# Five staging buffers for the modulation weights, and gated-linear outputs stored whole, in a hybrid GLA and retention layer

## The chip, the cores and the metric

The kernel runs on one core of one Trainium2 chip. The metric is device time in microseconds of one execution. The kernel before takes 1753.43 us, the median of 3 runs (1752.35 to 1753.49). All arithmetic is float32; matmul operands are stored as pairs of a rounded high part and the remainder, so that one product becomes three matmuls (high by high, low by high, high by low).

## The reference

One layer with two parallel branches over 1024 prompt tokens and 8 x 4 sample tokens (32 beside the prompt, 1056 in all), model width 1024. Cut to what matters:

```python
shift, scale, gate = split(c @ w_ada + b_ada, 3)        # modulation, 9 conditions: prompt, 8 samples
h = x * (1 + scale) + shift
qg, kg, vg, zg, lr, qr, kr, vr, zr, mg, mr = split_in(h @ w_in)
o_g, s_gla_new = gla(qg * GLA_DK**-0.5, kg, vg, log_alpha, s_gla)   # 4 heads, dk 128, dv 256
o_g = head_rmsnorm(o_g) * gla_norm_g * silu(zg)                     # "gated-linear output"
o_r, s_ret_new = retention(rotary(qr), rotary(kr), vr, s_ret)       # 4 heads, dk 256, dv 512, chunks of 128
o_r = head_groupnorm(o_r) * ret_norm_g * silu(zr)
merged = sigmoid(mg) * (o_g @ w_branch_gla) + sigmoid(mr) * (o_r @ w_branch_ret)
y = layernorm(DEEPNORM_ALPHA * x + gate * (merged @ w_out))
```

The outputs are y and both new states, for prompt and sample.

## The kernel before, in words

**Three stages.** `project` computes `h @ w_in`, `attend` the retention branch, the branch products and the rest. The line numbers are those of the profile of the kernel before.

**The start of `project`.** x (transposed) is in eight tiles `xt` of [128, 2, 528]; two of them (j and j + 4) make one quarter of the operands. For each of the eight tiles a piece of the modulation weights (`ada`, 1 MB in two DMAs of 512 KB) is loaded by SP (`load_ada`, three buffers in turn), PE makes the modulation product of 8 matmuls (`ada`, L508), ACT copies it (`fin`, `mod`, L514), PE transposes it (L517), DVE adds the bias, and `hcalc` scales and shifts the x tile (two small DVE operations and one ACT operation, L527). `combos` then makes the operands from two scaled tiles: the projection multiplies 2 x 2 blocks by a scheme of seven products (P1 to P7), each of which needs its own sum of x blocks. There are seven operands `XH[i]`/`XL[i]`: high part by ACT (`hi`, L541), remainder by DVE (`lo`, L545), sums by DVE (`sums`, L537, in tiles `S`). `first(j)` multiplies one quarter of P2, P1 and P5 as soon as it is there. A loop of eleven rounds writes this in order: modulation product i, copy and scaling of tile i - 1, half of the combos of a pair, the next loads.

**The loop of the projection.** 44 groups of weight columns (NG), seven products each, in the order P2, P1, P5, P6, P3, P4, P7. A group has four blocks of raw weights (`load_raw`, L135, SP), four sums of them (`tsum`, L146, POOL), and each product's weights are split into `wh`/`wl` three products ahead (`parts`, L94/L95 by `split`). PE runs it at L169 (`prod`); ACT and DVE take the results out of PSUM (`outs`, `C` tiles) after P1, P5, P6, P3, P4 and P7, and later functions store the columns.

**Work laid beside the projection.** From group NP1 on, `Q.units`, a list of small functions for the gated linear attention (`gla_units`), is run beside the products: `want` says how many of them must be done after product n, so that all are done 12 products ahead of the end. Its function `gated` transposes the normed output, multiplies it by the gate (`of`), splits it (`ox`, 32 prompt and 4 sample blocks) and stores both parts to DRAM (`og_d[0]`, `og_d[1]`). After the last unit `Q.late` is opened, the list of `early`: loads for the first retention head, its first scores (A0), two copies, and `R.SP`, which prepares the sample tokens' operands (`kd`, `kdr`, `vst`, `A4r`). One of them is run after every second product; what is left runs after the last.

**The junction to `attend`.** `attend` opens its pools, loads the two parts of the gated-linear outputs (4.3 MB each) from DRAM by four POOL DMAs into `og` (four of six `o4` buffers), and calls `begin()` of `branch`, which loads and splits the first branch weights (`wunit`: SP DMA L1195, split). `stage` then runs the retention head in eight chunks of 128 tokens and fills PE with the branch products (`fill`, L1238 to L1240, 352 columns each). For each chunk a retention state of the samples is split by ACT and POOL (`spl`, `ar`), `C1` and `C2` compute scores and output (`o`), `S0` is the first sample product (it reads `A4r` and `vst`). In every chunk but the first head's first, `spl` comes ahead of C1.

**What sets the order.** Each engine runs its instructions in the order in which the code writes them, and waits on semaphores for the others; DMAs of a queue are issued in the order in which their engine reaches them. A buffer of a pool is written again once its last readers are done; a pool that is opened over a closed one waits for the tiles that lay there.

Of the kernel before, what the change touches and what calls it, by code (L numbers as in the profile page):

```python
# [18 lines left out]
P = 128  # L19
# [26 lines left out]
def hybrid_step(ctx: ExitStack, tc: tile.TileContext, a: dict):  # L46
# [44 lines left out]
    og_d = [dp.tile([P, 8, TA], F32, name=f"ogd{i}") for i in range(2)]  # L91
# [16 lines left out]
    def project(early):  # L108
        with ExitStack() as cx:
            xp = pool(cx, "xp")  # L110
            wp = pool(cx, "wpb")
            ps = cx.enter_context(tc.tile_pool(name="psb", bufs=1, space=PSUM))
            _project(xp, wp, ps, early)

    def _project(xp, wp, psp, early):
        XH, XL = {}, {}
        for i in (1, 3, 2, 5, 4, 0, 6):
            XH[i] = xp.tile([P, 4, HT], F32R, name=f"xh{i}")
            XL[i] = xp.tile([P, 4, HT], F32R, name=f"xl{i}")
        mem = SimpleNamespace(cx=None, pool=None, bufs=0)  # L120

        def open_mem(name, bufs):
            mem.cx = ExitStack()
            mem.pool = pool(mem.cx, name)
            mem.bufs = bufs
# [367 lines left out]
        open_mem("su", 0)  # L493
# [38 lines left out]
        def sums(j, k):  # L532
            h0, h1 = xs[j], xs[j + 4]
            x, y, op = {1: lambda: (h0[:, 1], h1[:, 1], add), 2: lambda: (S[1], h0[:, 0], sub),
                        4: lambda: (h1[:, 0], S[2], sub), 3: lambda: (h0[:, 0], h0[:, 1], sub)}[k]()
            S[k] = sup.tile([P, HT], F32, tag="S", name="S", bufs=2)
            nc.vector.tensor_tensor(S[k], x, y, op=op)  # L537

        def hi(j, *ops):
            for i, src in ops:  # L540
                nc.scalar.activation(XH[i][:, j, :], src, AF.Copy)  # L541

        def lo(j, *ops):
            for i, src, eng in ops:
                eng.tensor_tensor(XL[i][:, j, :], src, XH[i][:, j, :].bitcast(F32), op=sub)  # L545

        def combos(j, half):
            h0, h1 = xs[j], xs[j + 4]
            V = nc.vector
            if half == 0:  # L550
                hi(j, (1, h1[:, 0]), (0, h0[:, 0]))
                sums(j, 1)
                lo(j, (1, h1[:, 0], V))
                hi(j, (4, S[1]))
                lo(j, (0, h0[:, 0], V))
                sums(j, 2)
                lo(j, (4, S[1], V))
            else:
                hi(j, (5, S[2]), (3, h1[:, 1]))
                lo(j, (3, h1[:, 1], V))  # L560
                sums(j, 4)
                lo(j, (5, S[2], V))
                hi(j, (2, S[4]))
                sums(j, 3)
                lo(j, (2, S[4], V))
                hi(j, (6, S[3]))
                lo(j, (6, S[3], V))

        nc.vector.tensor_scalar(bada[:, 1, :], bada[:, 1, :], 1.0, None, op0=add)
        for i in range(3):  # L570
            load_ada(i)
            load_x(i)
            if i == 1:
                load_raw(0, ((1, 0), (0, 0), (0, 1), (1, 1)))
# [10 lines left out]
        for i in range(11):  # L585
            if i < 8:
                ada(i)
                if i + 3 < 8:
                    load_ada(i + 3)
            if 0 < i <= 8:  # L590
                fin(i - 1)
            if i == 1:
# [4 lines left out]
            if i >= 3:  # L597
                combos(seq[(i - 3) // 2 * 2], (i - 3) % 2)
            if 0 < i <= 8:
                hcalc(i - 1)  # L600
                if i + 2 < 8:
                    load_x(i + 2)
            if i % 2 == 0 and i > 3:
                first(seq[i - 4])
# [19 lines left out]
        for n, (g, i) in enumerate(flat):  # L624
# [30 lines left out]
            if Q.late:  # L655
                if n % 2 and Q.late[0]:
# [973 lines left out]
```

## Time and profile before

| | before |
|---|---|
| median of 3 runs | 1753.43 us |
| the profiled execution | 1751.33 us |
| its span (first to last instruction) | 1749.6 us |
| PE busy | 1671.3 us |
| mean granted PE clock | 0.984 |

The profile is of one execution. Busy times count an instruction from its start to its end; the share of an engine is its busy time by the span. The page cuts the span into 40 slices of 43.7 us and prints each engine's busy share in tenths. A group's row gives line, engine, operation, tile written from tiles read, count, busy time and mean ns, then the idle time ahead of it and what ended it. "PEclk" or the clock of a window is the granted clock of TensorE, 1.00 at full speed. "SPq" and "POOLq" rows are DMAs issued by those engines' queues, with the time in which they were under way. The engine and page rows that the argument needs stand in the prediction.

### The profile page before, as it was taken

The numbers are of one execution on the slowest core, as the hardware profiler recorded it, in microseconds if no ns is written. First come the engines' busy times: TensorE is split into PE (matmuls) and PEld (weight loads), VectorE is DVE, ScalarE is ACT, GpSimd is POOL, SyncE is SP. The second block draws the span as 40 slices with busy tenths as digits, with TensorE's granted clock in tenths as the row PEclk, the third lists the DMA queues.
The fourth block names the chain that finished last, engine by engine and source line by source line (L and its number), as shares of the span: only waits on it lengthen the run. The fifth ranks groups of instructions, "written<-read, shape, count | busy, mean of one in ns | idle before, by whom it ended". The sixth has DMA issues, their size and how long they took to land.

```text
span 1749.6 us, 32388 instructions
## 1 busy us (share of the span) xinstructions
PE 1671.3 (96%) x11848; PEld 1552.5 (89%) x11848; DVE 1150.3 (66%) x2278; ACT 840.5 (48%) x1819; POOL 697.8 (40%) x791
## 2 busy tenths in 40 slices
PE   7899989999999999999999999799999999998997
PEld 4799989999999999999999999699898788887775
DVE  4647777677765666656576555365676878877557
ACT  4556555543335656556565555333355545434201
POOL 1115656334443343333333332132334444445516
PEclk9999999999999999999999999799999999999998
DMA  8213434543336555555554545766655555447613
GB/s 320 95 50 129 139 127 152 166 137 127 114 113 165 160 165 149 164 148 144 172 152 144 159 146 196 284 193 193 201 159 167 170 171 169 147 123 230 208 37 113
DMA packets 242671, 275.41 MB, mean 157 GB/s; under 512 B 54147, under 2 KB 171472, under 8 KB 242000
## 3 DMA queue, kind: packets, MB, share of 16 engines
q1 hardware_dynamic: 226288, 216.27, 39.9%
q0 software_dynamic: 11872, 48.42, 8.7%
q10 hardware_dynamic: 4352, 8.65, 1.4%
q8 instruction: 93, 1.52, 0.4%
q14 instruction: 66, 0.54, 0.1%
HBM read 176.80 MB, written 96.47 MB: 156 GB/s over the span
## 4 chain that ended last, share of the span: by engine, by line
PE 38%; DVE 4%; POOL 4%; DMA 4%; issue 3%; ACT 2%; POOLq 0%; DVEq 0%; ACTq 0%; SPq 0%
PE psA L169 6%; PE psC L169 4%; PE mm L1239 3%; PE mm L1238 3%; PE mm L1240 3%; PE aux L738 3%; PE o L738 3%; PE psB L169 2%; PE psD L169 2%; PE mm L1453 1%; PE mm L1455 1%; PE mm L1454 1%; PE so L1132 1%; DMA wraw<-wo 1%; POOL acc L1400 1%
## 5 line engine op out<-in xcount | busy, mean ns | idle before, releaser
L169 PE MATMUL psA<-xh,wh 128*128 128x264 f32 x1056 | 306.0, 290 | 8.4 <-ACT C L205 4.7
L169 PE MATMUL psA<-xl,wh 128*128 128x264 f32 x1056 | 301.0, 285 | 1.0 <-DVE xl L545 1.0
L169 PE MATMUL psA<-xh,wl 128*128 128x264 f32 x1056 | 301.4, 285 | 0.5 <-DVE wl L95 0.5
L146 POOL TENSOR_TENSOR T<-raw 128x512 f32<-128x512 f32 x88 | 126.1, 1433 | 214.9 <-DVE wl L95 188.7
L169 PEld LDWEIGHTS psA<-xh,wh 128*128 128x128 f32 x1056 | 199.9, 189 | 12.0 <-ACT C L205 5.8
L146 POOL TENSOR_TENSOR T<-raw,T 128x512 f32<-128x512 f32 x88 | 119.3, 1356 | 226.1 <-issue 161.0
L169 PE MATMUL psC<-xh,wh 128*128 128x264 f32 x704 | 201.9, 287 | 0.3 <-ACT C L210 0.3
L169 PEld LDWEIGHTS psA<-xl,wh 128*128 128x128 f32 x1056 | 200.2, 190 | 1.2 <-DVE xl L545 1.2
L169 PEld LDWEIGHTS psA<-xh,wl 128*128 128x128 f32 x1056 | 200.0, 189 | 0.8 <-DVE wl L95 0.7
L169 PE MATMUL psC<-xl,wh 128*128 128x264 f32 x704 | 199.8, 284 | 0.5 <-DVE xl L545 0.5
L169 PE MATMUL psC<-xh,wl 128*128 128x264 f32 x704 | 200.0, 284 | 0.0
L94 ACT ACTIVATE wh<-raw 128x512 fp32r<-128x512 f32 x180 | 113.0, 630 | 150.7 <-PE psC L169 43.1
L95 DVE TENSOR_TENSOR wl<-raw,wh 128x512 fp32r<-128x512 f32 x180 | 135.9, 755 | 60.8 <-ACT wh L94 57.1
L95 DVE TENSOR_TENSOR wl<-T,wh 128x512 fp32r<-128x512 f32 x176 | 125.4, 713 | 62.9 <-ACT wh L94 58.0
L94 ACT ACTIVATE wh<-T 128x512 fp32r<-128x512 f32 x176 | 110.7, 629 | 105.9 <-PE psA L169 72.5
L1238 PE MATMUL mm<-oh,wh 128*128 128x352 f32 x384 | 128.1, 334 | 7.6 <-DVE acc L1398 6.0
L169 PEld LDWEIGHTS psC<-xh,wh 128*128 128x128 f32 x704 | 132.5, 188 | 1.5 <-issue 0.8
L169 PEld LDWEIGHTS psC<-xl,wh 128*128 128x128 f32 x704 | 132.6, 188 | 0.7 <-DVE xl L545 0.7
L169 PEld LDWEIGHTS psC<-xh,wl 128*128 128x128 f32 x704 | 132.6, 188 | 0.0
L95 POOL TENSOR_TENSOR ar<-s0p,ar 128x512 fp32r<-128x512 f32 x64 | 83.6, 1306 | 107.1 <-ACT ar L94 105.8
L1240 PE MATMUL mm<-oh,wl 128*128 128x352 f32 x384 | 124.8, 325 | 0.0
L1239 PE MATMUL mm<-ol,wh 128*128 128x352 f32 x384 | 124.6, 324 | 0.0
(313 smaller groups left out, 4640.2 us busy)
## 6 DMA issues: line engine op xcount, KB each, us to landing
raw<-wx SPq DMA_DIRECT2D x176, 256.0 KB, 3.1
s0p<-state_ret POOLq DMA_DIRECT2D x32, 512.0 KB, 4.5
o_srs<-s0p POOLq DMA_DIRECT2D x32, 512.0 KB, 3.9
raw<-wb SPq DMA_DIRECT2D x48, 256.0 KB, 3.9
thd<-C ACTq DMA_DIRECT2D x16, 528.0 KB, 3.6
og<-ogd POOLq DMA_DIRECT2D x4, 2112.0 KB, 11.5
thl<-thd SPq DMA_DIRECT2D x48, 176.0 KB, 3.4
ada<-wada SPq DMA_DIRECT2D x16, 512.0 KB, 7.1
```

The costliest lines, as they stand in the source:

```text
L94: nc.scalar.activation(hi, src, AF.Copy)
L95: (eng or nc.vector).tensor_tensor(lo, src, hi.bitcast(F32), op=sub)
L146: nc.gpsimd.tensor_tensor(t, x, y, op=sub)
L169: nc.tensor.matmul(ps[:, :SUB], w[:, j, :], x[:, j, c], start=start and j == 0 and i == 0, stop=stop and j == 3 and i == 2, skip_group_che ...
L738: nc.tensor.matmul(out, lhs(l), rhs(r), start=start and i == 0, stop=stop and i == 2)
L1132: nc.tensor.matmul(R.po[:64], qp[:, d].rearrange("p l t -> p (l t)"), R.ar[:, l, :], start=False, stop=b == 7 and d == 1 and l == 1)
L1238: nc.tensor.matmul(ps, wh[:, j, :], oh[:, j, g0:g1], start=first, stop=False)
L1239: nc.tensor.matmul(ps, wh[:, j, :], ol[:, j, g0:g1], start=False, stop=False)
L1240: nc.tensor.matmul(ps, wl[:, j, :], oh[:, j, g0:g1], start=False, stop=last)
L1400: nc.gpsimd.tensor_tensor(A, A, m0, op=add)
L1453: nc.tensor.matmul(ps, xh, wh[:, k, :], start=k == 0, stop=False)
L1454: nc.tensor.matmul(ps, xh, wl[:, k, :], start=False, stop=False)
```

## The change

The diff does four things.

1. **Start.** Two more buffers for modulation weights (`ada3`, `ada4` in a pool `more`); five pieces and four x tiles are asked for ahead of the first product, in turn. The pool is closed in round 4; operand 6 (`xh6`, `xl6`) and the projection's weight buffers (`wpb`) are placed there afterwards, so the first raw weights, their sums and the first three weight splits move from rounds 0 and 1 to round 4. The combos are made in pieces, their sums in place (in one `S` tile, and the last in the x tile itself). The operands' quarters of pairs 2 and 3 come after the loop of now eight rounds, with `first(2)` and `first(3)`.
2. **Pace at the end of the projection.** The units are spread to be done 13 products ahead of the end instead of 12; the list of `early` has three rests and one function is taken after every product.
3. **Gated-linear outputs.** `gated` stores `of` as it is (one tensor `og_d`, two buffers of `of`), without a split. `attend` loads it by eight POOL DMAs of 528 KB into two `ograw` tiles and splits each eighth into `og` behind `begin()`, ahead of the first head's `stage`. The tiles `oh`/`ol` of the first head come after that, in the buffers of `ograw`.
4. **`kst` and S0.** `kst` moves to another pool (`wc`), and the first head's `S0` stands behind C1 and C2 of its first chunk.

```diff
-    og_d = [dp.tile([P, 8, TA], F32, name=f"ogd{i}") for i in range(2)]
+    og_d = dp.tile([P, 8, TA], F32, name="ogd")
...
+        operands(xp, (1, 3, 2, 5, 4, 0))
...
+        cy = ExitStack()
+        more = pool(cy, "more")
         def load_ada(i):
-            r = raws[i] = sup.tile([P, 2, 4, 256], F32, tag="ada", name="ada", bufs=3)
+            if i % 5 < 3:
+                r = sup.tile([P, 2, 4, 256], F32, tag="ada", name="ada", bufs=3)
+            else:
+                r = more.tile([P, 2, 4, 256], F32, name=f"ada{i}")
+            raws[i] = r
...
+            if what == 0:
+                hi(j, 1, h1[:, 0])
+                hi(j, 0, h0[:, 0])
+                s = S[j] = sup.tile([P, HT], F32, tag="S", name="S", bufs=2)
+                ssum(s, h0[:, 1], h1[:, 1], add)
+                lo(j, 1, h1[:, 0])
+                hi(j, 4, s)
+                lo(j, 0, h0[:, 0])
+                lo(j, 4, s)
+            elif what == 5:
+                ssum(S[j], S[j], h0[:, 0], sub)
+                hi(j, 5, S[j])
+                lo(j, 5, S[j])
...
+        for i in range(8):
+            ada(i)
+            if i + 5 < 8:
+                load_ada(i + 5)
+            if i:
                 fin(i - 1)
+            if i == 4:
+                cy.close()
+                operands(pool(cx, "xp6"), (6,))
+                wp = pool(cx, "wpb")
+                load_raw(0, ((1, 0), (0, 0), (0, 1), (1, 1)))
                 tsum(0, 1)
                 for k in range(3):
                     parts(0, k)
                 tsum(0, 2)
             if i >= 3:
+                j = (i - 3) // 2
+                for w in ((0,), (5, 2, 3, 6))[(i - 3) % 2]:
+                    combos(j, w)
+            if i:
                 hcalc(i - 1)
+            if i < 4:
+                load_x(i + 4)
+            if i in (4, 6):
+                first(i // 2 - 2)
...
+        fin(7)
+        hcalc(7)
+        first(2)
+        combos(3, 0)
+        first(3)
+        for w in (5, 2, 3, 6):
+            combos(2, w)
+            combos(3, w)
...
-                if n % 2 and Q.late[0]:
+                if Q.late[0]:
...
-                want = min(len(Q.units), len(Q.units) * (n + 1 - Q.first) // (len(flat) - Q.first - 12))
+                want = min(len(Q.units), len(Q.units) * (n + 1 - Q.first) // (len(flat) - Q.first - 13))
...
-                of = wk.tile([P, 2, n], F32, tag="of", name="of", bufs=1)
+                of = wk.tile([P, 2, n], F32, tag="of", name="of", bufs=2)
                 nc.vector.tensor_tensor(of, pv, z, op=mult)
-                ox = wk.tile([P, 2, 2, n], F32R, tag="ox", name="ox", bufs=1)
-                split(ox[:, 0], ox[:, 1], of)
-                for i in range(2):
-                    for sl, d0 in dsts:
-                        nc.sync.dma_start(og_d[i][:, 2 * h:2 * h + 2, d0:d0 + sl.stop - sl.start],
-                                          ox[:, i, :, sl].bitcast(F32))
+                for sl, d0 in dsts:
+                    nc.sync.dma_start(og_d[:, 2 * h:2 * h + 2, d0:d0 + sl.stop - sl.start], of[:, :, sl])
...
-            kst = AT.wb.tile([P, DK_R], F32R, tag="kst", name="kst", bufs=2)
+            kst = AT.wc.tile([P, DK_R], F32R, tag="kst", name="kst", bufs=2)
...
+        rest = lambda: None
+        return [loads, rest, rest, lambda: R.A0(0), rest, lambda: R.CPa(0), lambda: (R.CPv(0), R.ldv(2)), R.SP]
...
-            og = [[o4(f"og{i}{k}") for k in range(2)] for i in range(2)]
-            O = [(o4("oh"), o4("ol"))]
+            raw = [o4(f"ograw{k}", F32) for k in range(2)]
+            og = [[o4(f"og{i}{k}") for i in range(2)] for k in range(2)]
+            og = [[og[k][i] for k in range(2)] for i in range(2)]
...
-            for i in range(2):
-                for k in range(2):
-                    nc.gpsimd.dma_start(og[i][k].bitcast(F32), og_d[i][:, 4 * k:4 * k + 4, :])
+            for k in range(2):
+                for j in range(4):
+                    nc.gpsimd.dma_start(raw[k][:, j], og_d[:, 4 * k + j])
             begin()
+            for k in range(2):
+                for j in range(4):
+                    split(og[0][k][:, j], og[1][k][:, j], raw[k][:, j])
+            O = [(o4("oh"), o4("ol"))]
```

What moves, engine by engine. In the rows that follow, each line is an instruction with its line in the code, the tile written, the tile read, the shape and, where there are several in a row, how many; a number behind a name is that tile's in its own kernel.

**PE, the start.** `psada` is the modulation product (9x256) or its transposes (128x9), `psB` and `psA` the first quarters of P2 and P1; xh_129/xl_130 are operand 1 (P2) of the kernel before, xh_139 its operand 0 (P1). Before, the first place where operand matmuls stand, behind two modulation products:

```order
L517 MATMUL psada<-c_ident,mod 128x9 x4
L508 MATMUL psada<-ada,c_cT 9x256 x8
L169 MATMUL psB<-xh_129,wh 128x264
L169 MATMUL psB<-xl_130,wh 128x264
L169 MATMUL psB<-xh_129,wl 128x264
```

And now, with xh_125/xl_126 as operand 1:

```order
L518 MATMUL psada<-ada,c_cT 9x256 x8
L527 MATMUL psada<-c_ident,mod 128x9 x4
L518 MATMUL psada<-ada,c_cT 9x256 x8
L527 MATMUL psada<-c_ident,mod 128x9 x2
L518 MATMUL psada<-ada,c_cT 9x256 x8
L527 MATMUL psada<-c_ident,mod 128x9 x2
L173 MATMUL psB<-xh_125,wh 128x264
L173 MATMUL psB<-xl_126,wh 128x264
```

Before, the first operand matmuls stand behind the third modulation product and the other products between them; now all eight modulation products come first.

**ACT, the end of the start.** The rows from the last scaling of an x tile (L527, xt<-xt) to the first copy of a PSUM result after P6 (L205, C<-psA) of the first group; xh tiles are operands, `wh` weights. Before:

```order
L527 ACTIVATE xt<-xt,modT 128x2x512
L94 ACTIVATE wh<-raw 128x512
L541 ACTIVATE xh_129<-xt 128x528
L541 ACTIVATE xh_137<-S 128x528
L541 ACTIVATE xh_131<-xt 128x528
L94 ACTIVATE wh<-T 128x512
L541 ACTIVATE xh_135<-S 128x528
L94 ACTIVATE wh<-T 128x512
L541 ACTIVATE xh_133<-S 128x528
L541 ACTIVATE xh_141<-S 128x528
L205 ACTIVATE C_555<-psA 128x264 x2
```

Now, from the third copy behind the last scaling on (those ahead of it are wh<-T, xh_125<-xt and xh_135<-xt):

```order
L546 ACTIVATE xh_133<-S 128x528
L546 ACTIVATE xh_131<-S 128x528
L546 ACTIVATE xh_127<-xt 128x528
L94 ACTIVATE wh<-T 128x512
L546 ACTIVATE xh_131<-S 128x528
L546 ACTIVATE xh_129<-S 128x528
L94 ACTIVATE wh<-raw 128x512
L94 ACTIVATE wh<-T 128x512
L546 ACTIVATE xh_129<-S 128x528
L546 ACTIVATE xh_276<-xt 128x528
L94 ACTIVATE wh<-T 128x512
L209 ACTIVATE C_549<-psA 128x264 x2
```

Nine copies stood between the two places, and now fourteen do: the quarters of two pairs are made there instead of one.

**ACT, the junction.** `kdr`, `vst` and `A4r` come from R.SP, `kst` from the state's `prb`, `Sx` is the retention state's split, `ar` the sample state's, thd the last store of the projection. Before:

```order
L1093 ACTIVATE kd<-aux,c_rdw_s 32x256
L729 ACTIVATE vst<-aux 32x512
L728 ACTIVATE kdr<-kd 32x256
L729 ACTIVATE kdr<-kd 32x256
L252 ACTIVATE C_14688<-C_14688 128x528
L94 ACTIVATE wh<-raw 128x512
L254 DMA thd_115<-C_14688 128x2x528
L94 ACTIVATE wh<-raw 128x512 x2
L1114 ACTIVATE kst<-kdr,c_bmask_k 128x256
L94 ACTIVATE Sx<-S 128x512
```

Now:

```order
L220 ACTIVATE C_14583<-psD 128x264 x2
L1132 ACTIVATE kst<-kdr,c_bmask_k 128x256 x2
L256 ACTIVATE C_14583<-C_14583 128x528 x2
L258 DMA thd_115<-C_14583 128x2x528
L94 ACTIVATE wh<-raw 128x512 x2
L94 ACTIVATE og_14742<-ograw_14740 128x1056 x4
L94 ACTIVATE og_14744<-ograw_14741 128x1056 x3
L94 ACTIVATE Sx<-S 128x512 x2
L94 ACTIVATE og_14744<-ograw_14741 128x1056
L94 ACTIVATE wh<-raw 128x512
L94 ACTIVATE ar<-s0p 128x512
```

The copies of R.SP no longer stand between the last copies of PSUM and the branch weights; behind the first branch weights there are eight high parts of `ograw`, ahead of `Sx` and `ar`.

**SP, the first branch weights** (raw<-wb), with what each issue waits for. Before:

```order
L1077 DMA s_15679<-rsd_112 128x384 [waits DMAHW4_49]
L961 DMA rm<-rmask 128x128 [waits DMAHW5_49]
L971 DMA vt<-vd_79 128x4x128 [waits DMAHW7_49,PE_49]
L1195 DMA raw<-wb 128x512 [waits DVE_49,DMAHW1_49,PE_49,Pool_49]
L1195 DMA raw<-wb 128x512 [waits DMAHW2_49]
```

Now:

```order
L1095 DMA s_15548<-rsd_112 128x384 [waits PE_49]
L979 DMA rm<-rmask 128x128
L989 DMA vt<-vd_79 128x4x128 [waits DMAHW7_49,PE_49]
L1214 DMA raw<-wb 128x512 [waits DMAHW1_49,DVE_49,Pool_49]
L1214 DMA raw<-wb 128x512 [waits DMAHW2_49]
```

The first issue waited for PE as well as for a DMA, DVE and POOL, and now for the latter three only. PE's own rows between the first group's P6 and the last of the units are in the order of before, and again from the second chunk's output on.

More of the change, by code (lines that the diff above doesn't have):

```diff
@@ L110, in project, with _project, operands, open_mem @@
             xp = pool(cx, "xp")
-            wp = pool(cx, "wpb")
             ps = cx.enter_context(tc.tile_pool(name="psb", bufs=1, space=PSUM))
-            _project(xp, wp, ps, early)
-    def _project(xp, wp, psp, early):
+            _project(cx, xp, ps, early)
+    def _project(cx, xp, psp, early):
         XH, XL = {}, {}
-        for i in (1, 3, 2, 5, 4, 0, 6):
-            XH[i] = xp.tile([P, 4, HT], F32R, name=f"xh{i}")
-            XL[i] = xp.tile([P, 4, HT], F32R, name=f"xl{i}")
+        def operands(pl, which):
+            for i in which:
+                XH[i] = pl.tile([P, 4, HT], F32R, name=f"xh{i}")
+                XL[i] = pl.tile([P, 4, HT], F32R, name=f"xl{i}")
+        operands(xp, (1, 3, 2, 5, 4, 0))
+        wp = None
         mem = SimpleNamespace(cx=None, pool=None, bufs=0)
-        def open_mem(name, bufs):
+        def open_mem(name, bufs, side="left"):
             mem.cx = ExitStack()
-            mem.pool = pool(mem.cx, name)
+            mem.pool = pool(mem.cx, name, side)
             mem.bufs = bufs
@@ L543, in lo, with ssum @@
[L543 to L557, printed above, removed]
-            else:
[L559 to L567, printed above, removed]
+        def ssum(t, x, y, op):
+            nc.vector.tensor_tensor(t, x, y, op=op)
@@ new lines, in hi, with lo, combos @@
+        def hi(j, i, src):
+            nc.scalar.activation(XH[i][:, j, :], src, AF.Copy)
+        def lo(j, i, src):
+            nc.vector.tensor_tensor(XL[i][:, j, :], src, XH[i][:, j, :].bitcast(F32), op=sub)
+        def combos(j, what):
+            h0, h1 = xs[j], xs[j + 4]
+            if what == 0:
[11 more added lines that the diff above has]
+                lo(j, 5, S[j])
+            elif what == 2:
+                ssum(S[j], h1[:, 0], S[j], sub)
+                hi(j, 2, S[j])
+                lo(j, 2, S[j])
+            elif what == 3:
+                hi(j, 3, h1[:, 1])
+                lo(j, 3, h1[:, 1])
+            else:
+                ssum(h0[:, 1], h0[:, 0], h0[:, 1], sub)
+                hi(j, 6, h0[:, 1])
+                lo(j, 6, h0[:, 1])
@@ L569, in _project @@
         nc.vector.tensor_scalar(bada[:, 1, :], bada[:, 1, :], 1.0, None, op0=add)
-        for i in range(3):
+        for i in range(4):
             load_ada(i)
             load_x(i)
-            if i == 1:
-                load_raw(0, ((1, 0), (0, 0), (0, 1), (1, 1)))
+        load_ada(4)
         q0 = G[0]
@@ L1254, in F @@
                     state.f += 1
-            R.S0()
+            if R is not AT.first:
+                R.S0()
             for c in range(NCH):
```

29 lines of the change are left out of this document (4 added, 25 removed).

## The prediction

> **What bounds the kernel now.** I read the page first, then busy time by stage (the windows), then PE's waits, and then the timeline at the two places where PE stands still.
>
> ```profile
> PE 1671.3 (96%) x11848; PEld 1552.5 (89%) x11848; DVE 1150.3 (66%) x2278; ACT 840.5 (48%) x1819; POOL 697.8 (40%) x791
> PE   7899989999999999999999999799999999998997
> ```
>
> TensorE is the bound nearly everywhere; only slices 1 and 2 (the start) and slice 26 (between projection and attention) fall clearly below 9. A window row gives length, PE, PEld, DVE, ACT and POOL busy, granted clock, DMA share and GB/s:
>
> ```profile
> 10.00:20.00 10.00, 9.12 (x46) 4.15 (x44) 4.04 (x9) 4.10 (x7) 3.40 (x3) 1.00 1.03 403
> 50.00:60.00 10.00, 7.47 (x44) 5.17 (x42) 8.50 (x18) 7.62 (x12) 0.00 (x0) 1.00 0.13 46
> 60.00:70.00 10.00, 6.24 (x30) 5.82 (x30) 6.36 (x12) 4.49 (x10) 4.73 (x2) 0.68 0.08 26
> 500.00:600.00 100.00, 97.84 (x808) 96.01 (x807) 62.08 (x151) 50.74 (x133) 41.29 (x50) 1.00 0.54 157
> 600.00:700.00 100.00, 100.00 (x827) 98.52 (x827) 66.16 (x151) 58.24 (x149) 38.79 (x46) 1.00 0.53 154
> 1104.80:1110.00 5.20, 1.08 (x11) 0.70 (x10) 3.20 (x9) 3.99 (x9) 1.47 (x2) 0.82 1.01 397
> 1110.00:1115.00 5.00, 4.50 (x10) 3.04 (x10) 0.13 (x1) 0.00 (x0) 0.00 (x0) 0.51 1.03 395
> 1120.00:1125.00 5.00, 3.03 (x9) 2.15 (x9) 3.73 (x8) 3.73 (x9) 2.45 (x4) 0.50 0.99 293
> 1125.00:1130.00 5.00, 3.35 (x8) 1.85 (x7) 1.44 (x3) 1.08 (x2) 1.51 (x2) 0.50 0.56 193
> ```
>
> At the end of the start DVE and ACT are the busy ones. At the junction every engine is idle much of the time, the DMA engines are full (1.01 and 1.03), and the clock stands near 0.5.
>
> **The start.** A timeline row gives start, length, engine, line, instruction, and the idle time before it with what ended it:
>
> ```profile
> 6.14 8.47 PE L508 MATMUL psada<-ada,c_cT 128*9 128x256 f32 x32 [6.14 <-DMA ada<-wada]
> 36.02 0.97 SPq L503 DMA_DIRECT2D xt<-xT  x2
> 48.39 3.62 PE L508 MATMUL psada<-ada,c_cT 128*9 128x256 f32 x16
> 56.25 1.24 ACT L527 ACTIVATE xt<-xt,modT 128x1024 f32<-128x1024 f32 x1
> 64.42 0.65 ACT L205 ACTIVATE C<-psA 128x264 f32<-128x264 f32 x2
> 64.85 0.59 PE L169 MATMUL psA<-xh,wh 128*128 128x264 f32 x1 [3.28 <-ACT C L205]
> L541 ACT ACTIVATE xh<-S 128x528 fp32r<-128x528 f32 x16 | 10.2, 636 | 6.0 <-DVE S L537 6.0
> L545 DVE TENSOR_TENSOR xl<-xt,xh 128x528 fp32r<-128x528 f32 x12 | 8.4, 703 | 2.2 <-ACT xh L541 2.2
> L537 DVE TENSOR_TENSOR S<-xt 128x528 f32<-128x528 f32 x8 | 5.6, 705 | 2.9 <-ACT xt L527 2.8
> L514 ACT ACTIVATE mod<-psada 9x256 f32<-9x256 f32 x8 | 3.0, 370 | 16.1 <-PE psada L508 16.1
> ```
>
> The last modulation product starts at 48.39, the last scaled x tile is done at 57.49, and the first matmul of unbroken work, P6 of group 0, starts at 64.85. After the change PE does all eight modulation products (3.62 us each) before any operand matmul, in their new loads' order. Five of them and four x tiles are 5.2 + 2.2 MB, at 403 GB/s done near 22 us, ahead of PE. I walk the new order with these durations. The third product ends near 19.1, the fourth near 23.8. The fourth's 0.37 us copy stands in ACT's queue behind two scalings and four operand copies, so the fifth starts near 26.2 and the sixth ends at 33.4. The seventh ends at 38.4, and after a copy and a transpose of some 1.4 us together the eighth runs 39.9 to 43.5: 8.5 us earlier than 52.0. The last scaling of x, with DVE nearly full by then, is done near 49.3 instead of 57.5, 8.2 us earlier.
>
> The tail gets longer. Behind that scaling ACT now has fourteen copies before the L205 copies, against nine, because two of the four quarter blocks are left for the end and the first weight splits come late. DVE has fourteen instructions there which ACT's last copies hang on: 14 x 0.68 is 9.5 us, so 58.8, then one operand and one weight copy and L205: P6 starts near 59.8. That is **5 us less**, of the 8.2. The upper bound is 8 (the tail as long as before), the lower one -1 (three more copies of 0.37 us caught behind some 2 us of ACT work each). PE's pause ahead of P6 becomes about 6 us instead of 3.28; both end at a clock near half (0.68 on average in 60 to 70), so no difference is counted. The group's raw weights, moved in SP's queue behind the last two x loads, leave near 33 instead of 5 us; they're first read near 47, so that move costs nothing; it would cost what they were later than 47.
>
> **The junction.** It runs from the last projection matmul at 1104.81 to the second chunk's o at 1149.28, 44.5 us:
>
> ```profile
> 1104.81 0.31 PE L1083 MATMUL aux<-s 128*32 128x32 f32 x4
> 1104.83 13.49 SPq L1195 DMA_DIRECT2D raw<-wb  x5
> 1110.28 0.66 PE L1105 MATMUL so<-vst,A4r 128*64 128x512 f32 x1 [4.40 <-DVE vst L731]
> 1115.93 0.63 ACT L94 ACTIVATE wh<-raw 128x512 fp32r<-128x512 f32 x1 [6.43 <-DMA raw<-wb]
> 1129.48 0.50 PE L1239 MATMUL mm<-og,wh 128*128 128x352 f32 x1
> 1149.28 2.10 PE o L738 x9
> 1148.66 0.16 PE mm L1240
> 1151.38 0.22 PE aux L996 x2
> 1151.60 0.44 PE aux L1011 x4
> ```
>
> PE's own work in it is 108 matmuls of 352 columns (nine units of twelve), 25 of 512 columns and six transposes: 108 x 0.16 + 25 x 2.10/9 + 0.66, which is 23.8 us. Some 20 us are waits and a half clock. First PE waits 4.40 us for the sample operands, whose step (R.SP) stood last in the list of early work. Then it waits for the branch weights, 11.1 us under way from 1104.83 to 1115.9, behind the gated outputs:
>
> ```profile
> 1086.13 0.61 POOL L1341 DMA_DIRECT2D og<-ogd  x1 [0.25 <-PE psB L169]
> 1095.99 0.53 POOL L1341 DMA_DIRECT2D og<-ogd  x1 [2.61 <-PE psA L169]
> og<-ogd POOLq DMA_DIRECT2D x4, 2112.0 KB, 11.5
> s0p<-state_ret POOLq DMA_DIRECT2D x32, 512.0 KB, 4.5
> L338 ACT ACTIVATE e<-e x4: 1087/1094/1102, 120.8 to 237.8; 128x1056 f32<-128x1056 f32 x4
> L340 DVE TENSOR_TENSOR D<-D,e x4: 1257/1258/1260, 124.6 to 241.6; 128x1056 f32<-128x1056 f32 x4
> ```
>
> The change takes away three things. R.SP stands five steps (15 us) ahead of the end, so its chain lies under projection matmuls. The gated outputs are 4.3 MB instead of 8.7, in eight transfers bound to the last P2 and P1 of the projection, so at 395 GB/s they're in some 5 us before it ends. The branch weights no longer wait for PE's last matmul and are in before it too.
>
> It adds eight splits of 128x1056, ACT 8 x 1.09 and DVE 8 x 1.26 us, in both queues ahead of Sx and of the state splits ar. From the end of the projection (T): ACT does two kst copies, two tanhs, a DMA issue and two weight copies until T+4.2, so the first split is whole (both halves) near T+6.5 and PE can start on its upper half at T+5.3. PE has chunk 0's C1, C2, S0 and transposes until T+3.6, and then a pause of 1.7 us. Each split releases nine matmuls, 1.44 us, against 1.26 on DVE: PE is the slower of the two, and the 72 matmuls of the first block end near T+17. Behind the splits stand Sx, one weight copy and ar on ACT, then ar on POOL (1.3 us): T+16.5; a second ar comes near T+19 and makes PE wait about a us. The rest, some 36 matmuls of 352 columns and seven of 512, ends near T+28; with a few waits for DVE's backlog I take T+29.5. R.SP's 1.1 us of PE time went ahead of T. The gain is 44.5 - 29.5 - 1.1, **14 us**. The upper bound is PE's own work, 44.5 - 23.8 - 1.1, 20 us. The lower bound is half clock all through the splits: 11.5 us more for 72 matmuls, so 2 to 3 us.
>
> From the next instruction on PE's order is that of before, with one state fetch (4.5 us) well ahead of its use, so I carry the gain to the end.
>
> **In between.**
>
> ```profile
> L95 DVE TENSOR_TENSOR ox<-of,ox 128x256 fp32r<-128x256 f32 x32 | 18.0, 561 | 2.6 <-ACT ox L94 2.3
> L94 ACT ACTIVATE ox<-of 128x256 fp32r<-128x256 f32 x32 | 13.2, 412 | 6.0 <-DVE of L834 3.7 <-DMA ogd<-ox 2.3
> PE aux L832 <- ACT on L825: 1.8, 2, 1.6
> ```
>
> The small splits taken away are 13 us of ACT, 18 of DVE and half of the output stores, but PE is at 98 to 100% in those windows: 0 to 4 us, and I take 1. Units and early work at another pace cost PE nothing as long as its loads come; the early scores now follow the last output stores by 12 us instead of 18, with loads of some 4 us between.
>
> **The sum.** 5 + 14 + 1 is 20 us. The profiled execution took 1751.33 us (span 1749.6), so 1731.3; the runs' median is 2.1 us above it, so **1733 us**.
>
> **The clock, the row first.** After the pause of 4.40 us the clock was 0.51; in 50 to 60, with pauses of about a us, it was 1.00. The Trainium skill (TensorE: Matmul & The Clock Gate, "Part 1: The HAM clock gate") says that an idle window of about 3.4 us halves the clock and a busy one of that length restores it. By that rule a pause of 1.7 us does not halve it, and the trace agrees as far as its rows go; were the clock halved all the same, the page's rule would give it back after the first few us.
>
> **The rivals.** (1) Half clock at the junction: PE, fed in pieces, stays near 0.5 as in 1110 to 1130 and the splits cost it 11.5 us more: 1742 to 1745. For it: four windows at 0.5 to 0.83 with PE 36 to 90% busy. Against it: PE comes from full work, and each split feeds it longer than the next one takes. 12%. (2) The start gives nothing, the longer tail eating the 8 us: 1738, inside my range. 10%. (3) Slower: ACT and DVE take their queues in order, and the splits wait for the gated outputs, so if those land late, Sx, ar and every later chunk stand behind them. C2 of chunk 1 comes 24 us after PE's first matmul on a split, so the junction is lost from a first split at about T+19 on, and with the 6 us won elsewhere the kernel is slower from T+25; at T+33 it takes 1761. The loads, asked for 16 to 19 us ahead of T, would have to be over 40 us under way against 11.5 now. With all that could go so, 7%. (4) The change does not do what it says: the branch weights or R.SP still hang on the last matmul; the wait of 4.4 or of 6.4 us stays: 1738 to 1742, 8%. The forecast (1726 to 1738) keeps 63%.
>
> **Range.** 1724 (8 + 18 + 3) to 1746 (start nothing, junction 6, between 1). 0.2%, 3.5 us, is about what a measurement of this kernel can tell from no change: faster 0.88, same 0.05, slower 0.07.
>
> **What would show it.** P6 of group 0 starts near 59.8; the eighth modulation product near 40; no 4.4 us wait for vst; the first split of ograw right behind the second wh copy, some 4 us after the last projection matmul; clock 1.0 from there; o of chunk 1 about 30 us after that matmul; windows from 500 to 1100 as before. Wrong would be: a split that waits for DMA, a clock of 0.5 beside the splits, or a P6 later than 64.

## The result, and the profile after

The changed kernel takes 1737.93 us (median of 4 runs, 1736.22 to 1740.40) against 1753.46 us of before: a ratio of 0.9908, with a 95% interval of 0.9896 to 0.9921, which is 15.5 us less. The forecast was 1733. Run again beside later experiments it took 1735.76 us (ratio 0.9892, 0.9876 to 0.9909). The profiled execution took 1736.22 us, its span 1734.4, against 1751.33 and 1749.6.

The page of the changed kernel, busy time and PE's slices:

```profile
PE 1665.1 (96%) x11848; PEld 1552.0 (89%) x11848; DVE 1140.6 (66%) x2250; ACT 834.7 (48%) x1791; POOL 698.5 (40%) x795
PE   8899999999999999999999999899999999997997
PEclk9899999999999999999999999999999999999998
```

The start is no longer below 8, and the slice of the junction is an 8 instead of a 7. In a second profile of the same kernel the start reads 7 and 7 and the junction 9, so a step of one in a slice says little. The windows of the changed kernel around the end of the projection (length, PE, PEld, DVE, ACT, POOL, clock, DMA share, GB/s):

```profile
1095.00:1100.00 5.00, 5.00 (x44) 5.00 (x43) 0.86 (x2) 1.24 (x3) 0.00 (x0) 1.00 1.03 407
1100.00:1105.00 5.00, 4.04 (x32) 3.79 (x31) 1.54 (x4) 1.95 (x5) 1.18 (x2) 1.00 0.40 153
1105.00:1110.00 5.00, 3.64 (x19) 2.62 (x17) 4.55 (x10) 4.56 (x7) 2.11 (x3) 1.00 0.88 256
1110.00:1115.00 5.00, 4.45 (x28) 4.45 (x29) 5.00 (x5) 5.00 (x7) 0.00 (x0) 1.00 1.03 338
1120.00:1125.00 5.00, 2.99 (x16) 2.55 (x17) 4.68 (x8) 2.21 (x4) 4.07 (x3) 1.00 0.15 37
```

The DMA engines are full until about 1101 and nearly free from 1102 on (0.10 and less in windows of 1 us), before the last projection matmul; from 1105 the next loads fill them again. Behind that matmul DVE and ACT are the full ones, PE is busy most of the time, and the clock stays at 1.00 where it was near 0.5 before. PE's timeline of the changed kernel at the same place (start, length, instruction, idle time before it and what ended it):

```profile
1103.24 0.28 PE L173 MATMUL psA<-xh,wl 128*128 128x264 f32 x1
1104.48 1.62 PE L760 MATMUL aux<-vj,kn 128*128 128x512 f32 x6 [0.96 <-DVE C L223]
1108.03 0.75 PE L1257 MATMUL mm<-og,wh 128*128 128x352 f32 x3
1110.56 0.43 PE L1258 MATMUL mm<-og,wh 128*128 128x352 f32 x1 [1.77 <-DVE og L95]
1121.07 0.44 PE L1150 MATMUL so<-ar,qp 128*64 128x512 f32 x1 [1.67 <-POOL ar L95]
1124.13 0.44 PE L1150 MATMUL so<-ar,qp 128*64 128x512 f32 x1 [0.94 <-POOL ar L95]
1133.74 1.56 PE L760 MATMUL o<-Sx,qs 128*128 128x512 f32 x6
```

From the end of the last projection matmul (1103.52) to the second chunk's o it is 30.2 us; it was 44.2 by the same rows (the prediction has 44.5), and 29.5 had been forecast. The first branch matmul comes 4.5 us behind the projection (forecast 5.3). The forecast had a pause of 1.7 us ahead of that matmul, and there PE stands still for 0.1; the pause of 1.77 us comes three matmuls later, for the first low part, so the same length is chance. The two waits for `ar`, 2.6 us together, are longer than the one microsecond that was allowed for.

### The profile page after: what moved, and what is told of

Same layout as the page of the kernel before. It is cut to its first block, busy times and chain, and to the rows that moved or that the text cites. A ratio compares the mean times of both kernels' runs of the same rounds, so it can differ in the third digit from the quotient of the medians.

```text
span 1734.4 us, 32226 instructions
## 1 busy us (share of the span) xinstructions
PE 1665.1 (96%) x11848; PEld 1552.0 (89%) x11848; DVE 1140.6 (66%) x2250; ACT 834.7 (48%) x1791; POOL 698.5 (40%) x795
## 4 chain that ended last, share of the span: by engine, by line
PE 59%; DVE 4%; POOL 3%; ACT 2%; issue 2%; DMA 2%; SPq 0%; POOLq 0%; DVEq 0%; ACTq 0%
PE psA L173 13%; PE psC L173 8%; PE psD L173 4%; PE aux L760 4%; PE psB L173 4%; PE mm L1258 3%; PE mm L1257 3%; PE mm L1259 3%; PE o L760 3%; PE aux L800 2%; PE mm L1479 2%; PE mm L1481 2%; PE mm L1480 2%; PE so L1150 1%; POOL rs L102 1%
```

## The experiments

The intervals are those of the ratio to the kernel before, whose runs stood beside each. "The changed kernel" has 1737.93 us (ratio 0.9908) and 1735.76 us (0.9892). The kernel before had medians of 1752.80, 1754.41 and 1753.08 us beside the three groups of experiments, so between groups the ratios compare better than the times. "The junction" is the time from the end of the last projection matmul to the second chunk's o: 30.2 us in both profiles of the changed kernel.

**The start alone.** The first part of the change, on the kernel before (its main lines):

```diff
-        for i in range(3):
+        for i in range(4):
             load_ada(i)
             load_x(i)
...
-        for i in range(11):
+        for i in range(8):
+            ada(i)
+            if i + 5 < 8:
+                load_ada(i + 5)
```

> The kernel before with the new start alone. Theory (the gain of 2.9 us at P6 of group 0 is the start's, and grows to 4.3 us because one half-clock stretch behind P6 is shorter; some 2 us are then lost by half-clock stretches at two pauses near 170 and 220 us which both kernels have, as chance has it): P6 at 62 us, time 1749 to 1751.5, and the stretches near 170 and 220 may or may not be there. Rival (the new start itself causes the loss of 2 us near 170 and 220 us): the two stretches are there in every run of the new start and never in one of the old, time 1751. Rival (the start gives nothing by itself): within 1 us of before.

1750.77 us against 1752.80, ratio 0.9988 (0.9978 to 0.9997): 2.0 us less. P6 of group 0 started at 64.35 us in its profile, hardly earlier than 64.85 and not at the 62 expected (that execution, 1753.63 us, was the slowest of its twelve); the half-clock stretch near 170 was not there, the one near 223 was. The start gives about 2 us, and the two later stretches come and go.

**Everything but the start.** The second to fourth part, on the kernel before; against the changed kernel:

```diff
-        for i in range(4):
+        for i in range(3):
             load_ada(i)
             load_x(i)
...
-        for i in range(8):
+        for i in range(11):
```

> The changed kernel with the start of before: everything but the start. Theory (the junction gives 13 us, independent of the start): 13 us under before, 1740 to 1741; second chunk's o some 30 us behind the last projection matmul. Rival (part of the junction's gain is the start's, by where the clock's windows fall): 10 us or less.

1739.88 us, ratio 0.9928 (0.9917 to 0.9940): 12.9 us less. With the 2.0 us of the start that is 14.9, the change's 15.5 within the spread: the two halves add up. In its profile the junction took 33.4 us instead of the 30 expected, 6.8 of them at half clock.

**The pace alone.**

```diff
-                if n % 2 and Q.late[0]:
+                if Q.late[0]:
...
-        return [loads, lambda: None, lambda: R.A0(0), lambda: R.CPa(0), lambda: (R.CPv(0), R.ldv(2)), R.SP]
+        return [loads, rest, rest, lambda: R.A0(0), rest, lambda: R.CPa(0), lambda: (R.CPv(0), R.ldv(2)), R.SP]
```

> The kernel before with the pace at the end of the projection alone (R.SP some steps ahead of the end, one function after every product, 13 for 12), the two split parts stored and loaded as before. Theory (two causes: the wait of 4.4 us for vst and R.SP's 1.1 us go with the pace, and the branch weights no longer come last behind 8.7 MB of gated outputs; the bytes themselves still end near the junction): 6 to 9 us under before. Rival (the bytes are what counts, the pace frees only a wait behind which the next one stands): 0 to 2 us. Rival (the pace is all): 13 us.

1752.77 us, ratio 1.0000 (0.9992 to 1.0009): nothing, where 6 to 9 us had been the theory. PE's timeline of this kernel:

```profile
1108.60 0.42 PE L1105 MATMUL so<-vst,A4r 128*64 128x512 f32 x1 [0.95 <-DVE C L219]
1122.33 0.80 PE L1130 MATMUL aux<-vst,kst 128*128 128x512 f32 x1 [11.25 <-ACT kst L1114]
```

The wait of 4.40 us for `vst` is gone as planned, and 11.25 us of another wait stand behind it: `kst` is queued on ACT behind the copies of the branch weights, which have not landed. One wait took the place of the other.

**All but the pace.** The lines above and the divisor of `want` as in the kernel before, the rest changed:

```diff
-                if Q.late[0]:
+                if n % 2 and Q.late[0]:
```

> The changed kernel with the old pace (12, one function of the early list after every second product, no rests), so that R.SP stands at the end again. Theory: the wait for vst is back but eight splits and S0 behind C1 and C2 hide part of it: 4 to 7 us over the changed kernel, 8 to 11 under before. Rival (the bytes are what counts): no more than 2 us over the changed kernel. Rival (the pace is all): 13 us over it, 2 to 3 under before.

1735.19 us, ratio 0.9901 (0.9888 to 0.9914): not slower than the changed kernel. My theory of 4 to 7 us fell. Its timeline has the old wait back:

```profile
1104.02 2.85 PE L760 MATMUL aux<-vj,kn 128*128 128x512 f32 x6 [4.40 <-DVE vst L753]
```

In time it costs nothing. The splits of the gated outputs, which PE needs next, run on ACT and DVE beside it; the junction took 32.6 us in this profile, 2.3 more than in the changed kernel, and 1.1 of these are R.SP's own work, which is done inside it here.

**The gated outputs in two parts, all else changed.** Here `gated` splits and stores twice, and four loads of 2112 KB bring 8.7 MB.

```diff
-                for sl, d0 in dsts:
-                    nc.sync.dma_start(og_d[:, 2 * h:2 * h + 2, d0:d0 + sl.stop - sl.start], of[:, :, sl])
+                split(ox[:, 0], ox[:, 1], of)
+                for i in range(2):
+                    for sl, d0 in dsts:
+                        nc.sync.dma_start(og_d[i][:, 2 * h:2 * h + 2, d0:d0 + sl.stop - sl.start],
+                                          ox[:, i, :, sl].bitcast(F32))
```

> The changed kernel with the gated outputs split, stored and loaded in two parts as before; new start, pace, place of kst and S0 as changed. The branch weights' first load waits for PE no more here. Theory (the bytes and the wait for the last of the four large loads carry the junction): the gated outputs land some 5 to 8 us behind the end of the projection, PE waits for them, 7 to 11 us over the changed kernel: 1745 to 1749. Rival (what counts is that the branch weights no longer wait for PE's last matmul): within 3 us of the changed kernel, 1735 to 1741.

1748.19 us, ratio 0.9965 (0.9953 to 0.9978): 12.4 us over the changed kernel run beside it, which is nearly all of the junction's gain. It is still some 4 us under the kernel with the start alone (ratio 0.9988): pace, `kst` and S0 together are worth something here, and no run takes them apart. The three first loads of branch weights, by issue and by time from issue to landing, in the kernel before:

```profile
L1195 SPq DMA_DIRECT2D raw<-wb x3: 333/438/452, 1104.8 to 1105.7; - x3
DMA to landing us min/median/max: 11.1/11.3/11.5
```

in the changed kernel:

```profile
L1214 SPq DMA_DIRECT2D raw<-wb x3: 333/428/707, 1085.9 to 1086.8; - x3
DMA to landing us min/median/max: 7.1/9.8/11.4
```

and here:

```profile
L1218 SPq DMA_DIRECT2D raw<-wb x3: 339/423/617, 1085.9 to 1086.7; - x3
DMA to landing us min/median/max: 27.3/29.6/30.4
```

Issued at the same time as in the changed kernel, the weights land at 1113 to 1117 instead of by 1098, as late as when they were issued 19 us later, and PE waits for them:

```profile
1113.89 1.25 PE L1261 MATMUL mm<-og,wh 128*128 128x352 f32 x3 [6.05 <-ACT wh L94]
```

Three of the four large loads were issued 1.5 to 9 us behind the weights and landed at 1099, 1105 and 1111, before them. So the early issue bought the weights nothing here.

**kst in its old pool.** The first load of branch weights then waits for PE's last matmul again.

```diff
-            kst = AT.wc.tile([P, DK_R], F32R, tag="kst", name="kst", bufs=2)
+            kst = AT.wb.tile([P, DK_R], F32R, tag="kst", name="kst", bufs=2)
```

> The changed kernel with kst in its old pool, all else as changed. The branch weights' first load waits for PE's last matmul again by its semaphores. Theory (the move of kst is what lets the branch weights come early; a load of 256 KB takes 3 to 4 us where nothing is ahead of it, and half of it is hidden behind C1, C2 and the first half split): first weights some 6 us behind the last matmul, 2 to 5 us over the changed kernel: 1739 to 1743. Rival (the weights are worth all of the junction): 8 to 12 us over. Rival (nothing, the splits are later anyway): within 1.5 us.

1737.72 us, ratio 0.9905 (0.9889 to 0.9921), 2.0 us over the changed kernel beside it (0.9892, 0.9876 to 0.9909). The intervals overlap, so between nothing and 2 us is not settled by the times; in its profile the junction took 30.9 us, 0.6 more than in the changed kernel. The weights were issued at 1103.8 and landed within 2.8 to 6.9 us: with the queues nearly empty, being late costs little.

**Twice the bytes.** Behind each load of an eighth a second load of the same eighth into the tile that its split writes afterwards.

```diff
                     nc.gpsimd.dma_start(raw[k][:, j], og_d[:, 4 * k + j])
+                    nc.gpsimd.dma_start(og[0][k][:, j].bitcast(F32), og_d[:, 4 * k + j])
```

> The changed kernel with twice the bytes of the gated outputs: behind the load of each eighth into ograw stands a second load of the same eighth into the tile that its split writes afterwards (8.7 MB instead of 4.3, the result of the second load is overwritten). Stores, splits, pace, start and kst as changed. Theory (the bytes carry the junction: the branch weights, the first splits and the sample states all arrive behind them): the first split ends some 10 to 14 us behind the last projection matmul, 7 to 13 us over the changed kernel: 1744 to 1750. Rival (what counts is that the loads are eighths, taken one by one): the first split is hardly later, 0 to 3 us over.

1750.30 us, ratio 0.9987 (0.9978 to 0.9996), as much as the start alone gives: the junction's gain is gone. PE's timeline, and the three first loads of branch weights:

```profile
1123.70 0.79 PE L1148 MATMUL aux<-vst,kst 128*128 128x512 f32 x1 [12.52 <-DVE kn L1017]
L1214 SPq DMA_DIRECT2D raw<-wb x3: 333/423/426, 1088.3 to 1089.2; - x3
DMA to landing us min/median/max: 5.3/5.5/5.7
```

The branch weights are not late here. They land 5.3 to 5.7 us after their issue, sooner than in the changed kernel, although 8.7 MB are loaded again. So it was not the bytes alone that held them back in the two-part kernel: four loads of 2112 KB (16.5 KB of each partition) did it, and sixteen of 528 KB (4.1 KB) did not. Whether that is the size of the loads, their rows or their spacing in time, no run separates.

What is late here is the eighths themselves (the last lands at 1116.5 instead of 1102.5), the sample states (1121.5 instead of 1110.2) and the fourth load of weights (1121.9 instead of 1113.2). ACT waits 8.99 us for that load, and the copy that PE's 12.52 us hang on stands behind it. Both kernels with 8.7 MB lose the gain, each by another operand. What they share, and the changed kernel does not, is that the loads are still under way when the projection ends. The order of ACT's queue differs in this kernel too: the copy of these weights stands ahead of the last six splits, so how much of the loss is the bytes' and how much the order's is open.

**The sample states' low parts on DVE.** POOL's rows for `ar` in the changed kernel, with DVE's beside it:

```profile
1116.97 4.05 POOL L95 TENSOR_TENSOR ar<-s0p,ar 128x512 fp32r<-128x512 f32 x1 [7.21 <-ACT ar L94]
1118.60 1.29 DVE L95 TENSOR_TENSOR Sx<-S,Sx 128x512 fp32r<-128x512 f32 x2
1119.80 1.22 DVE L1040 SCALAR_TENSOR_TENSOR rs<-mv,rs 128x1 f32<-128x1 f32 x1
```

POOL's split took 4.05 us where 1.3 is usual: it got through when DVE's last split ended at 1119.89, and then a DVE operation on 128 x 1 took 1.22 us until POOL was done at 1121.02.

```diff
-            split(R.ar[:, 0], R.ar[:, 1], R.sb[b][0][:, d, :], nc.gpsimd)
+            first = R is AT.first and b == 0
+            split(R.ar[:, 0], R.ar[:, 1], R.sb[b][0][:, d, :], nc.vector if first else nc.gpsimd)
```

> The changed kernel with the low part of the first chunk's two sample state splits on DVE instead of POOL. Theory (POOL's first one took 4.05 us, against 1.3 us as a rule, because DVE held the memory port that both use until its last split of the gated outputs ended; on DVE it takes 0.7 us): PE's wait of 1.67 us for ar goes to about 0.3 and the second of 0.94 away, 1 to 2.5 us under the changed kernel. Rival (DVE's queue is the bound there, so 1.4 us more on it delay all behind it): 0 to 1.5 us over.

1732.63 us, ratio 0.9872 (0.9856 to 0.9888), 3.1 us under the changed kernel beside it, though the intervals overlap. The junction took 28.7 us in this profile, and again with both edits below: 1.5 us less, within the 1 to 2.5 expected. Where the other half of the 3.1 us comes from is not shown. The waits of 1.67 and 0.94 us are gone:

```profile
1116.12 0.39 PE L1151 MATMUL so<-ar,qp 128*64 128x512 f32 x1
```

**The last two weight sums of group 0 on DVE.** P6 waits for ACT's copies out of PSUM (L209), and in ACT's queue a weight copy stood right ahead of them. In the changed kernel:

```profile
59.28 1.65 POOL L150 TENSOR_TENSOR T<-raw 128x512 f32<-128x512 f32 x1 [6.91 <-DVE wl L95]
59.72 1.77 DVE L549 TENSOR_TENSOR xl<-xt,xh 128x528 fp32r<-128x528 f32 x1
60.96 0.63 ACT L94 ACTIVATE wh<-T 128x512 fp32r<-128x512 f32 x1 [1.36 <-POOL T L150]
61.92 0.39 PE L173 MATMUL psA<-xh,wh 128*128 128x264 f32 x1 [3.27 <-ACT C L209]
```

The copy is that of P7's weights, and waits for POOL's sum; POOL and DVE hold each other up (1.77 us for a remainder that takes 0.70). The same rows, POOL's sum and P6, in the changed kernel run again, where the sum lost the race:

```profile
58.88 2.79 POOL L150 TENSOR_TENSOR T<-raw 128x512 f32<-128x512 f32 x1 [6.91 <-ACT xh L546]
62.67 0.59 PE L173 MATMUL psA<-xh,wh 128*128 128x264 f32 x1 [4.86 <-ACT C L209]
```

and in the kernel with `ar` on DVE, where it won it:

```profile
58.48 1.27 POOL L150 TENSOR_TENSOR T<-raw 128x512 f32<-128x512 f32 x1 [6.91 <-DVE wl L95]
60.73 0.39 PE L173 MATMUL psA<-xh,wh 128*128 128x264 f32 x1 [2.12 <-ACT C L209]
```

```diff
-            nc.gpsimd.tensor_tensor(t, x, y, op=sub)
+            (nc.vector if g == 0 and i > 2 else nc.gpsimd).tensor_tensor(t, x, y, op=sub)
```

> The changed kernel with the last two weight sums of group 0 on DVE instead of POOL. Theory (P6 starts 2 us later than forecast because ACT's weight copy for P7 stood ahead of the copies for P6 and waited for POOL's sum, and because two DVE splits took 1 us longer each beside POOL's sums): P6 at 59.5 to 60.5 instead of 61.9, 1.5 to 2.5 us under the changed kernel. Rival (DVE is full there, two more operations of 0.7 us on it take all of it back): P6 at 61.5 to 62.5, no gain.

1730.14 us, ratio 0.9874 (0.9861 to 0.9888): by the ratios 3 us under the second measurement of the changed kernel, with which the interval overlaps, and 6 under the first; 1.5 to 2.5 had been expected. P6 started here, with ACT's rows beside it:

```profile
60.10 0.65 ACT L209 ACTIVATE C<-psA 128x264 f32<-128x264 f32 x2
60.52 0.39 PE L173 MATMUL psA<-xh,wh 128*128 128x264 f32 x1 [1.00 <-ACT C L209]
62.35 0.63 ACT L94 ACTIVATE wh<-T 128x512 fp32r<-128x512 f32 x1 [1.04 <-DVE T L150]
```

That is inside the theory's 59.5 to 60.5 but for 0.02. P7's weight copy (62.35) now stands behind the copies that P6 waits for, so the edit moved it in ACT's queue as well as the sum to DVE. That the copy's wait held P6 is shown; whether the faster sum or the new order took it away is not. With a pause of 1.00 us no half-clock stretch follows P6, and in this profile there was none near 170 either. How much of the 3 to 6 us is the edit and how much these runs' luck is open.

**Both edits.**

> The two edits together: the two weight sums of group 0 and the low parts of the first chunk's two sample states on DVE. Theory (two places that have nothing to do with each other): the gains add up, 3 to 5 us under the changed kernel, 1730 to 1734 and below ar_dve by 1 to 2. Rival (run to run chance of the clock hides it): within 1 us of ar_dve.

1727.70 us (1726.40 to 1728.86), ratio 0.9858 (0.9843 to 0.9873): the fastest of all, 25 us under before and by the ratios 6 to 9 under the changed kernel, more than the 3 to 5 expected.

**The changed kernel again, for the clock.**

> The changed kernel once more, beside the next three. Theory (times differ from run to run by where the pauses near 170 and 220 us fall in a fixed grid of 3.41 us in which the clock is granted): median 1736 to 1739, single runs from 1734 to 1741; in its profile every half-clock stretch follows a 3.41 us stretch of the grid in which PE was idle for more than about 1.5 us, and ends behind one in which it was hardly idle. Rival (the spread has another cause): half-clock stretches behind stretches with less idle time, or off the grid.

1735.76 us, just under the 1736 to 1739 expected; single runs 1733.97 to 1737.04. In all profiles the granted clock changes on a fixed grid of 3.41 us. These are windows cut on that grid, two pairs of neighbours in the changed kernel:

```profile
168.16:171.57 3.41, 1.59 (x13) 1.39 (x12) 3.18 (x6) 2.35 (x5) 1.03 (x1) 1.00 0.35 95
171.57:174.99 3.42, 3.42 (x18) 3.42 (x17) 3.42 (x9) 0.82 (x3) 1.28 (x1) 0.50 0.89 279
215.95:219.36 3.41, 1.28 (x11) 1.06 (x9) 2.56 (x5) 0.81 (x2) 0.00 (x0) 1.00 0.76 208
219.36:222.77 3.41, 2.73 (x12) 2.70 (x12) 3.03 (x5) 1.77 (x4) 1.28 (x1) 0.50 0.27 65
```

and, at the second of these places, in the kernel before:

```profile
217.23:220.64 3.41, 2.40 (x20) 2.19 (x19) 3.41 (x7) 0.00 (x0) 0.00 (x0) 1.00 0.50 140
220.64:224.06 3.42, 1.61 (x12) 1.51 (x12) 2.19 (x4) 2.58 (x5) 1.08 (x1) 1.00 0.58 157
224.06:227.47 3.41, 2.35 (x19) 2.24 (x19) 2.52 (x6) 1.55 (x3) 1.08 (x2) 1.00 0.56 204
```

The pause of 2.8 us is in both kernels. In the changed one it leaves PE 1.28 us busy in one window, and the next two are at half clock; in the kernel before the grid cuts it in two, PE is busy for 2.40 and 1.61 us, and nothing follows. Over all thirteen profiles, 66 windows at full clock had 1.9 us or more of idle PE time, and each was followed by half clock. Of windows with 1.5 to 1.9 us it was 16 of 28, and of some 6300 with less, 5. So the theory's 1.5 us is where half clock begins to be likely, and not a sharp line. Half clock ended behind 74 of the 76 windows in it that had less than 0.4 us of idle time, and behind none of the 73 with more.

The junction shows the same. Its pause was 1.77 us in the first profile of the changed kernel and 1.75 in the second; these are the windows around it, first in the one, then in the other:

```profile
1106.83:1110.24 3.41, 1.81 (x11) 1.17 (x9) 3.41 (x9) 3.41 (x5) 1.82 (x2) 1.00 0.92 306
1110.24:1113.65 3.41, 3.10 (x19) 3.10 (x20) 3.41 (x4) 3.41 (x4) 0.00 (x0) 1.00 1.02 347
1109.00:1112.42 3.42, 1.51 (x9) 0.98 (x7) 3.42 (x8) 3.42 (x5) 1.83 (x2) 1.00 0.96 309
1112.42:1115.83 3.41, 3.41 (x14) 3.41 (x13) 3.41 (x4) 3.41 (x5) 0.00 (x0) 0.50 0.98 320
```

## Why the prediction was right, and where it was not

The profiled pair differs by 15.2 us of span, 20 were forecast. Matched instruction by instruction, the changed kernel is ahead by 2.9 us at P6, by 3.9 at 75 us, by 4.4 at 170, by 2.2 at 233, by 2.4 at 700, by 15.4 at the second chunk's o and by 15.2 at the end.

- **The start: 5 us forecast, 2.9 at P6.** All eight modulation products ran first, the last started at 39.26 (forecast 39.9), and the last scaling of x was done at 49.26 (forecast 49.3): up to there the walk was right. The step that failed is "one operand and one weight copy and L205: P6 starts near 59.8". These copies were given 1.0 us in all; even without a wait they take 1.5 (from 59.05 to 60.52 in the kernel with the sums on DVE). And I did not ask what the weight copy waits for: POOL's sum for P7, beside a full DVE. P6 started at 61.92. In the other profiles with the new start and POOL's sums it started between 60.7 and 61.9 where that sum took 1.27 or 1.61 us, and between 62.3 and 64.75 where it took 2.79; with the old start it was 64.85, 63.84 and 65.42. So the 2.9 us of this pair are in part chance. In time the start alone is worth 2.0 us. Taking the sums off POOL brought P6 to 60.52. PE's pause ahead of P6 was 3.27 us as before, not the 6 of the forecast.
- **The junction: 14 us forecast, 13.0 between 700 us and the second chunk's o; 12.9 us in time for everything but the start.** Size and course were right but for the clock. Of the three things that the change was said to take away there, it is the gated outputs' loads that count: twice the bytes, or the two parts, give back 12 us or more; R.SP's earlier place is worth nothing in time, added alone or left out alone; the earlier issue of the branch weights 0 to 2 us, and nothing beside the four loads of 2112 KB. The forecast had nearly the right sum, since the waits were overlapping and it summed no prices but compared the end of the old chain with that of the new one. In part this was luck: a wait of 0.96 us for DVE ahead of C1 and the longer waits for `ar` were not in the sum, and the 1.5 us set aside for DVE's backlog covered most of them.
- **`ar`: 1.3 us forecast for POOL, 4.05 measured.** The row that the price came from (1306 ns mean) is of splits that run mostly without eight DVE splits in a row beside them.
- **In between: 1 us forecast, 0 found.** The lead is 2.2 us at 233 and 2.4 at 700; PE was the bound and the splits taken away bought nothing.
- **Half clock.** Behind P6 the stretch was 3.4 us instead of 6.8, which gave 1.0 us. At 171 the profile of the changed kernel had a stretch that the one of before lacked, which took 1.5, and the longer pause ahead of it 0.5. The stretch at 219 took some 2.2 us, but the kernel before lost 2.0 there to two waits for DVE, at 225 and 232. The forecast saw none of this.
- **The rivals.** Half clock at the junction did not come in the profiled run, but this was chance: the grid cut the pause, and the window with the larger part had 1.60 us of idle time, where run again it had 1.91. Of the eight profiles with the gated outputs loaded whole and once, the other seven all have half clock there, 3.4 us in six and 6.8 in one, and in four of them behind this same pause of 1.75 or 1.77 us. So the forecast's clock of 1.0 from there on was luck, and its step that a pause of 1.7 us does not halve the clock failed. The price was small, and not the 11.5 us of the rival: with 3.4 us the second profile of the changed kernel took 30.2 us all the same, with 6.8 the one without the start took 33.4. The start gave something, and the waits of 4.4 and 6.4 us went, so the second and fourth rival did not come. No split waited for a DMA, so the slower one did not come either.

Two statements ahead of the prediction do not hold. Instructions do not stand in an engine's queue wholly in the order in which the code is written: P7's weight copy is written behind the copies that P6 waits for, and stands ahead of them in ACT's queue. And these copies (L205, L209) take P1's result out of PSUM ahead of P6, not P6's after it.

## What to carry to other kernels

Price a transfer by the loads that are under way with it, not by when it is issued: beside four loads of 2112 KB an issue 19 us earlier arrived no earlier, beside loads of 528 KB it did. A wait that PE shows is worth its length only if nothing else it needs next comes as late: follow the next operand before counting the first. And follow each instruction in the queue ahead of the one that releases PE to its own source, above all where POOL and DVE work at the same time.

## What had not been expected of the hardware

- POOL and DVE stop each other: a sum on POOL took 1.27, 1.65 or 2.79 us, a split 4.05 instead of 1.3, and DVE operations next to them 1.77 instead of 0.70 and 1.22 us on 128 x 1. The Trainium skill says so (SBUF — State Buffer, "SBUF: two separate sides"): the two share a pair of ports under an exclusive lock, a DVE operation with two SBUF inputs takes it against a GpSimd one that reads SBUF, and the other waits for the whole instruction. The traces agree, and here the waiting one stood back for more than one instruction: POOL's 4.05 us spanned several DVE splits.
- The half clock follows a free-running grid. The Trainium skill (TensorE: Matmul & The Clock Gate, "Part 1: The HAM clock gate") gives its window as 3413 ns and says that it doesn't start with the kernel; the stretches of these profiles, whole multiples of 3.41 us but for those cut off by the end, agree. Its idle window is stricter than what the runs show: 1.82 us of idle time in one window were enough at 168 us (1.81 at 221 us in the kernel before were not), 1.9 us always were, and whether a given pause halves the clock depends on where the grid cuts it. At 171 us it made 1.5 us of difference between the two profiles; the runs of one kernel spread over 2 to 8 us, and that this is the main cause was not shown.
- 256 KB of weights took 27.3 to 30.4 us to land beside 8.7 MB in four loads of 2112 KB, 5.3 to 5.7 beside as many bytes in loads of 528 KB, and 2.8 to 6.9 with the queues nearly empty.
